# State space outputs behind twelve gate tiles, memory's norm behind all, projections sequence by sequence, lag 0 in one matmul with the other lags

## The chip, the cores and the metric

The kernel runs on one core of one Trainium2 chip. The metric is the device time of one execution in microseconds (us). A core has five engines, each with its own stream of instructions: TensorE (PE, the matmuls; PEld is its loading of weights), VectorE (DVE), ScalarE (ACT), GpSimd (POOL) and SyncE (SP, which here issues the transfers between HBM and the on-chip memory). An engine takes its instructions in order and waits on semaphores for what others produce.

## The reference

One encoder layer (DEPTH is 1) and a final norm, for two sequences ("prompt" and "sample", 512 tokens of 1024 features each) with a memory of 256 tokens each. The layer has three branches, a state space layer (S5), differential attention and cross attention over the memory; each goes through an up projection and a gate, their sum through an output projection; a gated feed-forward network follows.

```python
def _layer(x, mem, l, p):
    xn = _rmsnorm(x, p['norm_mix'][l])
    mn = _rmsnorm(mem, p['norm_mem'][l])
    h = xn @ p['w_in'][l]
    u, q, k, v, xq, g = jnp.split(h, IN_SPLITS, axis=-1)
    y_s5 = _s5_branch(u, ...)
    ...
    q = _partial_rope(q.reshape(Bn, L, 2 * DIFF_HEADS, DIFF_DH), cos, sin)
    k = _partial_rope(k.reshape(Bn, L, 2 * DIFF_HEADS, DIFF_DH), cos, sin)
    ...
    y_diff = _diff_attention(q, k, v, lam, p['diff_subln'][l], lambda_init)
    mk, mv = jnp.split(mn @ p['w_mem_kv'][l], 2, axis=-1)
    ...
    y_x = _cross_attention(xq.reshape(Bn, L, X_HEADS, X_DH), mk, mv)
    branches = (y_s5, y_diff, y_x)
    merged = None
    for n in range(N_BRANCH):
        term = jax.nn.sigmoid(g[..., n * D_MODEL:(n + 1) * D_MODEL]) * (branches[n] @ p['w_up'][l, n])
        merged = term if merged is None else merged + term
    x = x + merged @ p['w_out'][l]
    xn2 = _rmsnorm(x, p['norm_ffn'][l])
    gate, up = jnp.split(xn2 @ p['w_ffn_in'][l], 2, axis=-1)
    return x + (jax.nn.silu(gate) * up) @ p['w_ffn_out'][l]

def _s5_scan_dir(u, lam, step, b, c):
    lam_bar = jnp.exp(lam * step[:, None])
    b_bar = ((lam_bar - 1.0) / lam)[..., None] * b
    bu = jnp.einsum('lgh,gph->lgp', u.astype(jnp.complex64), b_bar)
    a = jnp.broadcast_to(lam_bar, bu.shape)
    _, xs = lax.associative_scan(_ssm_combine, (a, bu), axis=0)
    return jnp.real(jnp.einsum('lgp,ghp->lgh', xs, c))
```

The state space branch has 32 groups of 16 channels and 64 complex states, runs forward and backward in time, and ends with a gelu and a sigmoid gate of its own (w_glu).

## The kernel before, in words

**Precision.** All matrices are float32. For most products each operand is split into a high part (fp32r, which TensorE multiplies at full rate) and a low part, and three matmuls are made of one: low x with high weight, high with high, high x with low weight. `mm3` (lines 122 to 129) issues them for one slice k of 128 rows: for each sequence `xh` at line 126 and `xl` at line 127 with the weight's high part, then for each sequence line 129 with its low part. `weight` (lines 115 to 120) loads one 128x1024 tile of a weight matrix through a pool of two buffers; ScalarE makes the high part (line 109), VectorE the low part by a subtraction (line 110). `proj` (lines 131 to 137) makes one output tile of 128 features by 512 tokens for each of the two sequences: it takes two banks of PSUM, and in each step k it runs both sequences, three matmuls of 512 columns each. With 8 steps that is 48 matmuls for a tile of the gates or of the queries and keys, 24 for a tile of w_glu.

**The order of the stages.** Keys and values of the memory come first, then the norm of x and the input projection u of the state space branch (lines 277 to 291, written to memory and read back group by group). Then follow the gate tiles: 24 of them, each a `proj`, a tanh and a store (`gates`, lines 295 to 304). The state space branch is a Python generator, `s5_gen` (lines 893 to 1155); `next(s5)` issues its next stage between the gate tiles. `NG = (7, 10, 2)` says how many gate tiles stand between: seven, then memory's norm and the scan with its outputs, ten more, then the gelu of the state space outputs (lines 318 to 334), two more, then the four w_glu tiles (lines 338 to 346). The remaining five gate tiles stand in the attention stages (`NG_X`, `NG_D`). After w_glu come cross attention (lines 405 to 470), differential attention (`qk_tile`, lines 483 to 504, makes rotated queries and keys; `attend`, lines 506 to 546, one head of one sequence), the merging of the branches (`merge`, lines 551 to 599), the output projection, the feed-forward network (matmuls at lines 723 to 725) and the final norm. The attention stages take their projections' banks from two that are called mm, with three for scores and others for transposes (`open_banks` at the start of cross attention).

**What decides the order on an engine.** The program is built with a planner that simulates a timeline and moves instructions of one engine past one another where their data and buffers allow; the order of the Python code is its starting point, not the final order.

**Memory's norm** (lines 309 to 313): `sums` (lines 193 to 199) loads the four tiles of memN, squares them and sums them on TensorE; `factor` (lines 159 to 167) takes the square root on ScalarE, the reciprocal on VectorE (line 163), and spreads the four columns over the partitions by four transposes on TensorE (line 166); the results `mrs` and `mbc` are used in cross attention.

**The state space stages.** `cprod` (lines 1027 to 1035) makes complex products of a group's vectors with powers of its eigenvalues, six VectorE instructions for each block of eight groups. `input_weights` (lines 1038 to 1048) transposes them for the input matmuls. `output_weights` (lines 1056 to 1084) takes such products for eight lags in each direction (`Orf`, `Onf`, 128 columns a group), stores them in `cD`, and multiplies them on TensorE with the input vectors, which gives the kernel of the short-range lags: lines 1076 and 1077 make the 128 columns of the lags in plain float32, lines 1078 and 1079 the 16 columns of lag 0, from the vectors `cr` and `cn` themselves. The results go to `gD`. The scan (lines 1117 to 1123) carries the states over the 64 chunks of 8 tokens: 62 steps of four VectorE instructions. After it the outputs (lines 1125 to 1153): for each of four blocks of eight groups the stored products `c_r`, `c_n` and the lag matrix `w_` are loaded, ScalarE and VectorE copy a block's states into `x2` (one buffer), and TensorE makes 24 matmuls (lines 1146 to 1148), whose results are written to memory and read back by the gelu.

Of the kernel before, what the change touches and what calls it, by code (L numbers as in the profile page):

```python
# [10 lines left out]
F32 = mybir.dt.float32  # L11
# [24 lines left out]
NG = (7, 10, 2)  # L36
# [12 lines left out]
def encoder(ctx: ExitStack, tc: tile.TileContext, a, out):  # L49
# [34 lines left out]
    def bank(tag="mm"):  # L84
        return pools[tag].tile([P, 512], F32, tag=tag, name="bk" + tag)
# [35 lines left out]

    def mm3(outs, wh, wl, xs, k, nk):

        ws = slice(k * P, (k + 1) * P)
        for s, (xh, xl) in enumerate(xs):
            PE.matmul(outs[s], wh[:, ws], xh, start=(k == 0), stop=False)  # L126
            PE.matmul(outs[s], wh[:, ws], xl, start=False, stop=False)  # L127
        for s, (xh, xl) in enumerate(xs):
            PE.matmul(outs[s], wl[:, ws], xh, start=False, stop=(k == nk - 1))  # L129

    def proj(src, hi, lo, nk=KD, seqs=(0, 1)):

        wh, wl = weight(src, nk * P)
        outs = [bank() for _ in seqs]
        for k in range(nk):
            mm3(outs, wh, wl, [(hi[k][:, s * L : (s + 1) * L], lo[k][:, s * L : (s + 1) * L]) for s in seqs], k, nk)
        return outs
# [156 lines left out]

    def gates(n):

        for _ in range(n):
            t = next(todo)
            o = proj(a["w_in"][20 + t], xh, xl)
            gt = slot("ld", name="gt")  # L300
            for s in range(NS):
                cs = slice(s * L, (s + 1) * L)
                S.activation(out=gt[:, cs], in_=o[s], func=AF.Tanh, scale=0.5)
            nc.sync.dma_start(gD[t], gt)
# [3 lines left out]

    mrs = cst.tile([P, 4], F32, name="mrs")
    mbc = cst.tile([P, L], F32, name="mbc")  # L310
    rs_, bc = factor(sums(a["memN"], "ld"), DM)
    V.tensor_copy(mrs, rs_)
    S.copy(mbc, bc)
    next(s5)
    gates(NG[1])
    next(s5, None)
# [18 lines left out]
    gates(NG[2])  # L335
    bh = rp.tile([P, 4], F32, tag="bh", name="bh")
# [556 lines left out]
def s5_gen(k):  # L893
# [133 lines left out]
    def cprod(tag, ar, ai, xr, xi, sub):  # L1027

        o_r, o_i = slot(tag, sh4, name="cxr"), slot(tag, sh4, name="cxi")
        for o_, x1, x2, op in ((o_r, ar, ai, ALU.subtract if sub else ALU.add), (o_i, ai, ar, ALU.add if sub else ALU.subtract)):  # L1030
            t1 = slot(tag, sh4, name="ct1")
            V.tensor_tensor(out=t1, in0=x1, in1=xr, op=ALU.mult)
            V.tensor_tensor(out=o_, in0=x2, in1=xi, op=ALU.mult)
            V.tensor_tensor(out=o_, in0=t1, in1=o_, op=op)
        return tuple(o_.rearrange("p g e h -> p (g e h)") for o_ in (o_r, o_i))


    def input_weights(o):
        res = []
        for w_ in cprod("it", by_group(b_r, o), by_group(b_i, o), by_token(qr, o), by_token(qi, o), True):  # L1040
            t_ = slot("wb", [P, 8 * P], name="wb")
            for g4 in range(2):
                tr = aux()
                for g in range(4):
                    PE.transpose(tr[:, g * P : (g + 1) * P], w_[:, (4 * g4 + g) * P : (4 * g4 + g + 1) * P], ident)
                S.copy(t_[:, g4 * 512 : g4 * 512 + 512], tr)
            res.append(t_)
        return res
# [5 lines left out]
    cD = drp.tile([4, 2, P, 8 * 8 * 16], F32, name="cD")  # L1054

    def output_weights(o):
        Orf, Onf = cprod("it", by_group(cr, o), by_group(cn, o), by_token(xr_, o), by_token(xi_, o), False)
        nc.sync.dma_start(cD[o, 0], Orf)
        nc.sync.dma_start(cD[o, 1], Onf)
        for g4 in range(2):  # L1060
# [8 lines left out]
            for g2 in range(2):  # L1069
                kp = aux()  # L1070
                for g in range(2):
                    gg = 2 * g2 + g
                    lhr, lhi = lr48[:, gg, :], li48[:, gg, :]
                    cols = slice((4 * g4 + gg) * P, (4 * g4 + gg + 1) * P)
                    k1, k2 = kp[:48, g * 144 : g * 144 + P], kp[:48, g * 144 + P : (g + 1) * 144]
                    PE.matmul(k1, lhr, Orf[:, cols], start=True, stop=False)
                    PE.matmul(k1, lhi, Onf[:, cols], start=False, stop=True)
                    PE.matmul(k2, lhr, cr[:, hs.start + gg, :], start=True, stop=False)
                    PE.matmul(k2, lhi, cn[:, hs.start + gg, :], start=False, stop=True)
# [37 lines left out]
    for i in range(2, NC):  # L1117
# [5 lines left out]
        V.tensor_tensor(out=sv[:, :, :, i], in0=p_, in1=q_, op=ALU.add)  # L1123

    rt.close()
    k.open_tags(rt, side="right", x2=1, ow=6, sy=2)
    yv = k.yD.rearrange("(g h) j s c -> j h g (s c)", h=16)
    for o in range(4):
        gs = slice(8 * o, 8 * o + 8)
        c_r, c_n, w_ = (slot("ow", [P, 8, P], name=n_) for n_ in ("c_r", "c_n", "w_"))  # L1130
        nc.sync.dma_start(c_r.rearrange("p g q -> p (g q)"), cD[o, 0])
        nc.sync.dma_start(c_n.rearrange("p g q -> p (g q)"), cD[o, 1])
# [8 lines left out]
        for g4 in range(2):  # L1141
            ps = aux()
            for g in range(4):
# [3 lines left out]
                PE.matmul(d_, c_r[:, gg, :], x2[:, 0, 2 * gg : 2 * gg + 2, :].rearrange("p s c -> p (s c)"), start=False, stop=False)  # L1147
                PE.matmul(d_, c_n[:, gg, :], x2[:, 1, 2 * gg : 2 * gg + 2, :].rearrange("p s c -> p (s c)"), start=False, stop=True)
# [101 lines left out]
```

## Time and profile before

| What | Value |
|---|---|
| time, median of 3 runs | 1697.35 us (1695.62 to 1697.57) |
| time of the profiled execution | 1694.85 us |
| its span | 1693.0 us |
| mean granted clock of TensorE in it | 0.94 |
| moved by DMA | 196.66 MB, mean 116 GB/s |

The span runs from the first to the last instruction that the profiler recorded; the time has 1.85 us around it. "Granted clock" is the speed that the chip allowed TensorE, as a share of full speed. In the list of groups, a line such as "L126 PE MATMUL bkmm<-xh,wh 128x512 x640" names the line of the kernel, the engine, the operation, its output and inputs by the program's names, the shape, and how often it ran; behind the bar stand its summed busy time, the mean of one in ns, and the idle time of the engine just ahead of such instructions with what ended most of it. In a list of waits, "A <- B: 6.1, 4, 2.7" means that A waited for B for 6.1 us in all, in four waits, the longest 2.7. In a timeline each line begins with the start and the duration in us, and a bracket at its end gives the engine's idle time before it and what ended it. In a table by stretches, each line begins with the stretch and its length; then, for PE, PEld, DVE, ACT and POOL, the busy time and the number of instructions; then the mean granted clock, the share of the DMA engines' time and the GB/s moved.

### The profile page before, as it was taken

How to read it: one execution, taken by the hardware profiler on the slowest of the kernel's cores; microseconds unless marked ns; L12 is line 12 of the kernel's file. 1: busy time of each engine (PE TensorE's matmuls, PEld its weight loads, DVE VectorE, ACT ScalarE, POOL GpSimd, SP SyncE). 2: the span in 40 equal slices, each digit the busy share in tenths (PEclk: the TensorE clock that was granted, in tenths of full speed). 3: DMA queues.
4: the chain of work that ended last, by engine and by line, in shares of the span. 5: the costliest groups of instructions: out<-in, count | busy, mean ns of one | idle time of the engine just before them, and what ended most of it. 6: DMA issues, size and time to landing. Idle time of an engine off the chain costs nothing.

```text
span 1693.0 us, 21270 instructions
## 1 busy us (share of the span) xinstructions
PE 1631.7 (96%) x8044; PEld 1365.5 (81%) x8044; DVE 1086.8 (64%) x1788; ACT 620.1 (37%) x1092; POOL 391.0 (23%) x245
## 2 busy tenths in 40 slices
PE   5999998999999999999999999999999999999997
PEld 4788887887797778877888887888888888788887
DVE  7946897153554677778657659877777777753324
ACT  6534333243343446455422434222332323421121
POOL 0000000000000220210144345554555553500021
PEclk8999998999999999999999998999999999999998
DMA  9343262644112221315453541322222222742202
GB/s 363 112 151 117 92 211 103 197 176 174 47 51 75 69 69 51 112 46 160 154 188 119 152 134 63 112 100 88 75 88 75 88 87 98 237 148 66 77 22 100
DMA packets 79270, 196.66 MB, mean 116 GB/s; under 512 B 11072, under 2 KB 26688, under 8 KB 79168
## 3 DMA queue, kind: packets, MB, share of 16 engines
q1 hardware_dynamic: 79168, 195.31, 34.5%
q8 instruction: 63, 1.03, 0.3%
q14 instruction: 39, 0.32, 0.1%
HBM read 141.30 MB, written 49.77 MB: 113 GB/s over the span
## 4 chain that ended last, share of the span: by engine, by line
PE 67%; DVE 3%; ACT 2%; issue 1%; POOL 1%; DMA 1%; DVEq 0%; SPq 0%; POOLq 0%; ACTq 0%
PE bkmm L126 12%; PE bkmm L127 12%; PE bkmm L129 12%; PE bkmm L724 8%; PE bkmm L723 8%; PE bkmm L725 8%; DMA m<-m 1%; PE bksc L519 1%; PE bkmm L424 1%; PE bkmm L426 1%; PE bkmm L425 1%; PE bksc L520 1%; PE bktr L528 1%; POOL t L493 1%; DVE wl L110 0%
## 5 line engine op out<-in xcount | busy, mean ns | idle before, releaser
L109 ACT CAST wh<-wf 128x1024 fp32r<-128x1024 f32 (+4 forms) x164 | 142.3, 868 | 434.8 <-PE bkmm L127 278.8
L126 PE MATMUL bkmm<-xh,wh 128*128 128x512 f32 x640 | 252.8, 396 | 7.6 <-DVE t L491 3.0
L127 PE MATMUL bkmm<-xl,wh 128*128 128x512 f32 x640 | 251.8, 393 | 0.0
L724 PE MATMUL bkmm<-tl,wh 128*128 128x512 f32 x612 | 239.6, 391 | 2.9 <-DVE tl L110 2.9
L110 DVE TENSOR_TENSOR wl<-wf,wh 128x1024 fp32r<-128x1024 f32 (+4 forms) x164 | 182.5, 1113 | 92.0 <-ACT wh L109 91.1
L723 PE MATMUL bkmm<-th,wh 128*128 128x512 f32 x612 | 239.4, 391 | 0.0
L725 PE MATMUL bkmm<-th,wl 128*128 128x512 f32 x612 | 237.9, 390 | 0.0
L129 PE MATMUL bkmm<-xh,wl 128*128 128x512 f32 x640 | 224.1, 394 | 0.0
L126 PEld LDWEIGHTS bkmm<-xh,wh 128*128 128x128 f32 x640 | 120.9, 189 | 35.5 <-DVE t L491 5.5
L127 PE MATMUL bkmm<-al,wh 128*128 128x512 f32 (+1 forms) x408 | 147.0, 360 | 0.0
L126 PE MATMUL bkmm<-ah,wh 128*128 128x512 f32 (+1 forms) x408 | 147.0, 360 | 0.0
L492 POOL TENSOR_TENSOR t<-t,rs 128x512 f32<-128x512 f32 x16 | 21.9, 1368 | 518.1 <-DVE t L491 430.9
L127 PEld LDWEIGHTS bkmm<-xl,wh 128*128 128x128 f32 x640 | 121.1, 189 | 24.3 <-issue 0.2
L129 PEld LDWEIGHTS bkmm<-xh,wl 128*128 128x128 f32 x640 | 120.5, 189 | 24.4
L724 PEld LDWEIGHTS bkmm<-tl,wh 128*128 128x128 f32 x612 | 115.5, 189 | 28.4 <-DVE tl L110 4.6
L723 PEld LDWEIGHTS bkmm<-th,wh 128*128 128x128 f32 x612 | 115.5, 189 | 24.4 <-ACT th L109 0.3
L725 PEld LDWEIGHTS bkmm<-th,wl 128*128 128x128 f32 x612 | 115.1, 188 | 23.7
L129 PE MATMUL bkmm<-ah,wl 128*128 128x512 f32 (+1 forms) x408 | 127.4, 360 | 1.0 <-DVE wl L110 1.0
L788 POOL TENSOR_TENSOR up<-up,acc 128x512 f32<-128x512 f32 x44 | 85.1, 1956 | 148.0 <-DVE up L764 148.0
L848 DVE TENSOR_TENSOR y<-y,bkmm 128x512 f32<-128x512 f32 (+1 forms) x56 | 32.6, 609 | 110.8 <-PE bkmm L129 110.8
L146 POOL TENSOR_TENSOR acc<-acc,nsq 128x512 f32<-128x512 f32 (+1 forms) x32 | 37.9, 1186 | 242.4 <-ACT nsq L145 242.3
L129 PEld LDWEIGHTS bkmm<-ah,wl 128*128 128x128 f32 x408 | 76.9, 189 | 13.2 <-DVE wl L110 1.8
(586 smaller groups left out, 3293.9 us busy)
## 6 DMA issues: line engine op xcount, KB each, us to landing
wf<-in_w_in SPq DMA_DIRECT2D x40, 512.0 KB, 3.5
gD<-gt SPq DMA_DIRECT2D x24, 512.0 KB, 2.9
gl<-gD SPq DMA_DIRECT2D x24, 512.0 KB, 4.2
wf<-in_w_fg SPq DMA_DIRECT2D x22, 512.0 KB, 3.3
wf<-in_w_fu SPq DMA_DIRECT2D x22, 512.0 KB, 3.3
aD<-ac SPq DMA_DIRECT2D x22, 512.0 KB, 2.6
fl<-aD SPq DMA_DIRECT2D x22, 512.0 KB, 4.6
wf<-in_w_fo SPq DMA_DIRECT2D x16, 448.0 KB, 3.3
```

The lines of the kernel that those rows point to most:

```text
L109: S.copy(hi, src)
L110: V.tensor_tensor(out=lo, in0=src, in1=hi.bitcast(F32), op=ALU.subtract)
L126: PE.matmul(outs[s], wh[:, ws], xh, start=(k == 0), stop=False)
L127: PE.matmul(outs[s], wh[:, ws], xl, start=False, stop=False)
L129: PE.matmul(outs[s], wl[:, ws], xh, start=False, stop=(k == nk - 1))
L146: eng.tensor_tensor(out=acc[:, :n], in0=acc[:, :n], in1=sq[:, :n], op=ALU.add)
L492: PO.tensor_tensor(out=t2, in0=t2, in1=rope[1], op=ALU.mult)
L723: PE.matmul(ps, wh[:, ws_], th[:, o], start=(k == 0), stop=False)
L724: PE.matmul(ps, wh[:, ws_], tl[:, o], start=False, stop=False)
L725: PE.matmul(ps, wl[:, ws_], th[:, o], start=False, stop=(k == 3))
L788: PO.tensor_tensor(out=up, in0=up, in1=accs[s], op=ALU.mult)
L848: V.tensor_tensor(out=y[m][:, c : c + n], in0=y[m][:, c : c + n], in1=o_, op=ALU.add)
```

## The change

Five things are edited.

1. `proj` finishes the first sequence's eight steps before it begins the second's, and takes each bank when its sequence begins. The matmuls of a tile are the same in number.
2. `NG` becomes (7, 5, 7). The generator stops once more, after the scan, and its outputs are issued after twelve gate tiles, inside `with behind():`. `behind` returns `tc.issue_after(last_mm.ins)`: the instructions issued inside it may not be put ahead of the last matmul of the last `proj` before it. Seven gate tiles follow; in the code the gelu stands ahead of them.
3. Memory's norm moves from behind the seventh gate tile to behind all nineteen, also inside `behind()`.
4. Lag 0 is joined to the other lags. The product tiles of `output_weights` get a ninth slot of 16 columns for each group, into which GpSimd copies `cr` and `cn`; one pair of matmuls of 144 columns takes the place of a pair of 128 and a pair of 16. `cD`, `c_r` and `c_n` are 144 columns wide, and the output matmuls read their first 128.
5. `x2` has two buffers in place of one.

```diff
-NG = (7, 10, 2)
+NG = (7, 5, 7)
...
+    last_mm = None
     def mm3(outs, wh, wl, xs, k, nk):
+        nonlocal last_mm
         ws = slice(k * P, (k + 1) * P)
         for s, (xh, xl) in enumerate(xs):
             PE.matmul(outs[s], wh[:, ws], xh, start=(k == 0), stop=False)
             PE.matmul(outs[s], wh[:, ws], xl, start=False, stop=False)
         for s, (xh, xl) in enumerate(xs):
-            PE.matmul(outs[s], wl[:, ws], xh, start=False, stop=(k == nk - 1))
+            last_mm = PE.matmul(outs[s], wl[:, ws], xh, start=False, stop=(k == nk - 1))
     def proj(src, hi, lo, nk=KD, seqs=(0, 1)):
         wh, wl = weight(src, nk * P)
-        outs = [bank() for _ in seqs]
-        for k in range(nk):
-            mm3(outs, wh, wl, [(hi[k][:, s * L : (s + 1) * L], lo[k][:, s * L : (s + 1) * L]) for s in seqs], k, nk)
+        outs = []
+        for s in seqs:
+            cs = slice(s * L, (s + 1) * L)
+            outs.append(bank())
+            for k in range(nk):
+                mm3(outs[-1:], wh, wl, [(hi[k][:, cs], lo[k][:, cs])], k, nk)
         return outs
...
+    def behind():
+        return tc.issue_after(last_mm.ins)
...
     next(s5)
     gates(NG[0])
-
-    mrs = cst.tile([P, 4], F32, name="mrs")
-    mbc = cst.tile([P, L], F32, name="mbc")
-    rs_, bc = factor(sums(a["memN"], "ld"), DM)
-    V.tensor_copy(mrs, rs_)
-    S.copy(mbc, bc)
     next(s5)
     gates(NG[1])
+    with behind():
+        next(s5)
     next(s5, None)
...
     gates(NG[2])
+    with behind():
+        mrs = cst.tile([P, 4], F32, name="mrs")
+        mbc = cst.tile([P, L], F32, name="mbc")
+        rs_, bc = factor(sums(a["memN"], "ld"), DM)
+        V.tensor_copy(mrs, rs_)
+        S.copy(mbc, bc)
...
-        o_r, o_i = slot(tag, sh4, name="cxr"), slot(tag, sh4, name="cxi")
-        for o_, x1, x2, op in ((o_r, ar, ai, ALU.subtract if sub else ALU.add), (o_i, ai, ar, ALU.add if sub else ALU.subtract)):
+        tiles = [slot(tag, [P, 8, 8 if sub else 9, 16], name=n_) for n_ in ("cxr", "cxi")]
+        for o_, x1, x2, op in ((tiles[0], ar, ai, ALU.subtract if sub else ALU.add), (tiles[1], ai, ar, ALU.add if sub else ALU.subtract)):
+            o_ = o_[:, :, 0:8, :]
             t1 = slot(tag, sh4, name="ct1")
             V.tensor_tensor(out=t1, in0=x1, in1=xr, op=ALU.mult)
             V.tensor_tensor(out=o_, in0=x2, in1=xi, op=ALU.mult)
             V.tensor_tensor(out=o_, in0=t1, in1=o_, op=op)
-        return tuple(o_.rearrange("p g e h -> p (g e h)") for o_ in (o_r, o_i))
+        return tiles
     def input_weights(o):
         res = []
         for w_ in cprod("it", by_group(b_r, o), by_group(b_i, o), by_token(qr, o), by_token(qi, o), True):
+            w_ = w_.rearrange("p g e h -> p (g e h)")
...
-    cD = drp.tile([4, 2, P, 8 * 8 * 16], F32, name="cD")
+    cD = drp.tile([4, 2, P, 8, 144], F32, name="cD")
     def output_weights(o):
         Orf, Onf = cprod("it", by_group(cr, o), by_group(cn, o), by_token(xr_, o), by_token(xi_, o), False)
+        PO.tensor_copy(Orf[:, :, 8, :], cr[:, 8 * o : 8 * o + 8, :])
+        PO.tensor_copy(Onf[:, :, 8, :], cn[:, 8 * o : 8 * o + 8, :])
+        Orf, Onf = (o_.rearrange("p g e h -> p g (e h)") for o_ in (Orf, Onf))
         nc.sync.dma_start(cD[o, 0], Orf)
         nc.sync.dma_start(cD[o, 1], Onf)
...
-                    cols = slice((4 * g4 + gg) * P, (4 * g4 + gg + 1) * P)
-                    k1, k2 = kp[:48, g * 144 : g * 144 + P], kp[:48, g * 144 + P : (g + 1) * 144]
-                    PE.matmul(k1, lhr, Orf[:, cols], start=True, stop=False)
-                    PE.matmul(k1, lhi, Onf[:, cols], start=False, stop=True)
-                    PE.matmul(k2, lhr, cr[:, hs.start + gg, :], start=True, stop=False)
-                    PE.matmul(k2, lhi, cn[:, hs.start + gg, :], start=False, stop=True)
+                    k1 = kp[:48, g * 144 : (g + 1) * 144]
+                    PE.matmul(k1, lhr, Orf[:, 4 * g4 + gg, :], start=True, stop=False)
+                    PE.matmul(k1, lhi, Onf[:, 4 * g4 + gg, :], start=False, stop=True)
                 S.copy(gk[:, 2 * g2 : 2 * g2 + 2, :].rearrange("p g c -> p (g c)"), kp[:48, : 2 * 144])
...
         V.tensor_tensor(out=sv[:, :, :, i], in0=p_, in1=q_, op=ALU.add)
+    yield
     rt.close()
-    k.open_tags(rt, side="right", x2=1, ow=6, sy=2)
+    k.open_tags(rt, side="right", x2=2, ow=6, sy=2)
     yv = k.yD.rearrange("(g h) j s c -> j h g (s c)", h=16)
     for o in range(4):
         gs = slice(8 * o, 8 * o + 8)
-        c_r, c_n, w_ = (slot("ow", [P, 8, P], name=n_) for n_ in ("c_r", "c_n", "w_"))
-        nc.sync.dma_start(c_r.rearrange("p g q -> p (g q)"), cD[o, 0])
-        nc.sync.dma_start(c_n.rearrange("p g q -> p (g q)"), cD[o, 1])
+        c_r, c_n = (slot("ow", [P, 8, 144], name=n_) for n_ in ("c_r", "c_n"))
+        w_ = slot("ow", [P, 8, P], name="w_")
+        nc.sync.dma_start(c_r, cD[o, 0])
+        nc.sync.dma_start(c_n, cD[o, 1])
...
-                PE.matmul(d_, c_r[:, gg, :], x2[:, 0, 2 * gg : 2 * gg + 2, :].rearrange("p s c -> p (s c)"), start=False, stop=False)
-                PE.matmul(d_, c_n[:, gg, :], x2[:, 1, 2 * gg : 2 * gg + 2, :].rearrange("p s c -> p (s c)"), start=False, stop=True)
+                PE.matmul(d_, c_r[:, gg, 0:P], x2[:, 0, 2 * gg : 2 * gg + 2, :].rearrange("p s c -> p (s c)"), start=False, stop=False)
+                PE.matmul(d_, c_n[:, gg, 0:P], x2[:, 1, 2 * gg : 2 * gg + 2, :].rearrange("p s c -> p (s c)"), start=False, stop=True)
```

## The prediction, made before the changed kernel was run

> **What bounds the kernel now.** I read the page first, then the list of what PE waited for, then the timeline and stretches around the changed stages. Section 1, and the granted clock of section 2:
>
> ```profile
> PE 1631.7 (96%) x8044; PEld 1365.5 (81%) x8044; DVE 1086.8 (64%) x1788; ACT 620.1 (37%) x1092; POOL 391.0 (23%) x245
> PEclk8999998999999999999999998999999999999998
> ```
>
> TensorE (PE) is the bound: it is idle for only 61 us of 1693.0. A gain is therefore PE work taken away, a PE wait removed, or half-clock time avoided. The page shows 128x512 matmuls of 390 ns, but these overlap: in a full stretch they start every 0.227 us (925 to 1000 us holds 333). I use 0.227. What PE waited for, over the whole run (us, times, longest):
>
> ```profile
> PE bksc L519 <- DMA m<-m: 6.1, 4, 2.7
> PE bktr L166 <- DVE rs L163: 5.8, 3, 4.6
> PE bkmm L126 <- DVE t L491: 3.0, 5, 1.0
> ...
> PE bkmm L126 <- ACT sg L342: 1.3, 1, 1.3
> PE bkmm L126 <- DVE r L359: 1.2, 1, 1.2
> ```
>
> The 4.6 us is the memory norm (lines 309 to 313). PE's timeline there, then the stretches in which the clock was granted at half:
>
> ```profile
> 258.73 1.09 PE L166 MATMUL bktr<-ident,rs 128*128 128x128 f32 x4 [4.56 <-DVE rs L163]
> ```
>
> ```profile
> 256.89:263.70 6.81, 4.97 (x17) 4.42 (x18) 6.57 (x20) 0.59 (x1) 0.00 (x0) 0.50 0.22 77
> 434.38:437.78 3.40, 3.40 (x11) 2.72 (x11) 2.40 (x11) 1.02 (x4) 0.00 (x0) 0.50 0.46 159
> 762.06:765.46 3.40, 3.23 (x8) 2.29 (x9) 3.40 (x6) 3.00 (x4) 0.00 (x0) 0.50 0.77 229
> ```
>
> The reader sees that an idle stretch is paid twice: 4.56 us of waiting, then 4.97 us of work at clock 0.50 instead of 0.95, which is 4.97 x (1 - 0.50/0.95) = 2.4 us lost.
>
> **The change, part by part.** The order of both programs' instructions is the same up to the first lag matmuls (118 us) and again from the output projection on (920 us). Only the stretch between can change; the rest, 890 us, is taken as it is.
>
> *Lag 0 joined to the other lags (old lines 1074 to 1079).* One visit of PE to these matmuls, with the gate matmul after it:
>
> ```profile
> 212.51 0.42 PE L1076 MATMUL bktr<-cxr,lr 128*48 128x128 f32 x2
> 212.77 0.39 PE L1077 MATMUL bktr<-cxi,li 128*48 128x128 f32 x2
> 212.99 0.22 PE L1078 MATMUL bktr<-cr,lr 128*48 128x16 f32 x2
> 213.07 0.24 PE L1079 MATMUL bktr<-cn,li 128*48 128x16 f32 x2
> 213.16 0.40 PE L1076 MATMUL bktr<-cxr,lr 128*48 128x128 f32 x2
> ...
> 214.93 0.24 PE L1079 MATMUL bktr<-cn,li 128*48 128x16 f32 x2
> 215.10 0.50 PE L126 MATMUL bkmm<-xh,wh 128*128 128x512 f32 x1
> 215.44 0.39 PE L127 MATMUL bkmm<-xl,wh 128*128 128x512 f32 x1
> ```
>
> Each plain float32 matmul is two records. The two 16-column matmuls of a group cost 213.16 - 212.99 = 0.17 us, and there are 32 groups: 5.4 us go. The remaining 128 records grow from 128 to 144 columns; a record takes (212.99 - 212.77)/2 = 0.11 us, so an eighth is 0.014 us, and 128 of them 1.8 us. Net -3.6 us, on the path, because PE has no idle time from 118 to 250 us. Added are eight small copies on GpSimd (128x128 elements). The trace has none; the nearest rows are its memset of 128x192 (0.26 us, L1064) and its 128x512 sums (1.3 to 2.2 us, L492 and L493), so 0.3 to 0.6 us each. GpSimd is busy for 3.2 us of 118 to 254, so they hide, unless one stands ahead of a matmul that already waits (then 0.6 us each, 5 us at the worst). The sixteen transfers of cD grow by an eighth; landing takes 2.6 to 6.1 us, so 0.8 us more at most, hidden by loads that are issued tens of us ahead.
>
> *Fewer changes between kinds of matmul.* In the rows above, the first gate matmul after the visit holds PE for 215.44 - 215.10 = 0.34 us instead of 0.227, the last L1079 pair 0.17 instead of 0.09, and the edge before the visit costs about as much again in its two halves (0.09 and 0.04): 0.32 us a visit. Counting visits in the two orders, 219 changes of kind become 209, mostly because the output matmuls (lines 1146 to 1148) now stand in two blocks behind the twelfth and in the fourteenth gate tile, where before they were cut into about eight pieces. Five visits less: -1.6 us.
>
> *Memory's norm behind all gate tiles.* Its four transposes move into the second w_glu tile; with them go four loads of memN, four squares and two table loads on ScalarE, and a reciprocal. The wait of 4.6 and the half clock of 2.4 us go: -6.9. In the new place the square root follows the first half of the first w_glu output, and the transposes stand some 6.5 us of PE work behind that: table load 1.28, root 0.30, reciprocal 0.18, about 3 us to spare. Queued behind the loads on SP are the last gate's store and the fourth w_glu weight, which has 12 us of cover. Without that cover it would cost the same 4.6 again.
>
> *What the stall was hiding.* The scan (lines 1120 to 1123) fills VectorE from 182.6 to 282.7, and between its steps VectorE makes the low halves of the gate weights (L110):
>
> ```profile
> 257.06 1.22 DVE L110 TENSOR_TENSOR wl<-wf,wh 128x1024 fp32r<-128x1024 f32 x1
> ...
> 270.58 1.21 DVE L110 TENSOR_TENSOR wl<-wf,wh 128x1024 fp32r<-128x1024 f32 x1
> ```
>
> They come 13.5 us apart, while a gate tile is 48 x 0.227 = 10.9 us of PE. PE did not run into this because it stood still for the norm at 254. In the new order PE works without a break, so it does. The weight of the eleventh gate tile stands behind 17 more scan instructions (0.36 us each) and one more L110 (1.02 us net) than the one that started at 257.06: it starts at about 264.4 and is ready at 265.6. PE wants it at 264.7 (the last scan input ends at 181.4, then 82.9 us of PE work to that tile, then two matmuls): 0.9 late. The twelfth follows 34 scan instructions and one L110 later, ready at 278.8; PE wants it at 275.6 + 0.9: 2.2 more. So +3.1 us, from 0 (scan begins 3 us earlier) to 6 (3 us later). Next behind these: the outputs. The scan ends near 284 and its two copies (1.9 and 1.2 us) by 286; PE arrives near 289, so the outputs wait for nothing. Their own old waits for each other and for w (0.3 + 0.7) go: -0.7.
>
> *Projections one sequence, then the other.* Matmuls and weight loads are the same in number. What moves is when the first half is ready: 24 x 0.227 = 5.4 us earlier. At the start of cross attention PE waited for sg (1.27, bank not yet free), for qh (1.21) and for ql (0.52); counted in matmuls, the new order leaves 5.4 us between the first half and the first score, and over 2 us for the bank. So -3.0. The half clock at 434.38 followed those waits: 3.40 x 0.47 = -1.6, of which I take -1.0. In differential attention the waits on L491 and r (3.0 + 1.2) are two projections meeting at two banks; the shortest distances there are 0.2 to 1.9 us before, 0.9 to 1.9 after, and only three of them: -4.2. The score waits on the key's transfers (6.1) I leave as they are: bounds below.
>
> The Trainium skill's page "TensorE: Matmul & The Clock Gate" (section "HAM oscillation — how this bites in real kernels") says that the clock falls back after an idle stretch of about 3.4 us. This trace agrees at 4.56 us, but shows the half clock also at 434.38 and 762.06, where the longest single idle before it was 1.3 and 1.8 us. By the page alone the -1.0 would not be had and the sum would be 1 us smaller.
>
> **Sum.** -3.6 - 1.6 - 6.9 + 3.1 - 0.7 - 3.0 - 1.0 - 4.2 = -17.9 us. The profiled execution took 1694.85 us, a span of 1693.0; the new span would be 1675. The median of the runs shown is 1697.35, 2.5 above the profiled one; against it the forecast is 1679.5.
>
> **Rivals.** (a) The order by sequences does nothing in the attention stages: before, the trace at 609 to 614 us already runs L126, L127, L129 once each, so the planner had split the sequences wherever a bank was missing. For it: exactly that row. Against: the first cross projection was not split. The 4.2 stay: 1683.7. (b) VectorE paces the gates: the scan's lateness is 6 instead of 3.1, and its short idles gather into a half-clock stretch like the first above (6.81 x 0.47 = 3.2): 1685.6. Against: idles of 1 to 2 us, 11 us apart. (c) Slower: the key chain keeps its length while the planner moves the scores forward. Before, the first scores of the four heads stood 10.9, 16.0, 13.9 and 12.2 us of PE work behind their key projection and waited 0.9, 2.3, 0.2 and 2.7, so the chain took 11.8, 18.3, 14.1 and 14.9. Now they stand 10.9, 10.7, 10.2 and 9.2 behind. With the old lengths they wait 18.1 instead of 6.1, +12.0, three of the four long enough to halve the clock for 3 to 7 us (+6.0), and the 4.2 fall away: -17.9 + 22.2 = +4.3, so 1701.7. It decides once these waits exceed 24 us. Against: the 18.3 held 6 us in VectorE's queue and a transfer of 5.1 us behind a weight load; the bare chain (0.6, 0.7, 1.3, 2.2, 0.6, 2.3) is 8 us. (d) Better: the key waits vanish as well: 1673.4.
>
> **How the numbers follow.** Forecast 0.42, (a) 0.22, (b) 0.16, (c) 0.12, (d) 0.08. The range 1667 to 1697 takes in all but (c); its low end is (d) with the lateness at 0 and no more half clock at 762, its high end is (b) with the copies at 5 us and the key waits 6 us longer. A measurement of this kernel can tell 0.2%, 3.4 us, from no change: the upper ends of the forecast and of (b) (0.04) and the lower end of (c) (0.01) lie within it. Faster 0.84, same 0.05, slower 0.11.
>
> **What would show it.** No wait of L166 on L163 near 254 and no half clock there; L1078 and L1079 without successors; PE waiting for wl (L110) by 1 to 3 us between 264 and 280; the outputs in two blocks from about 289; no wait for sg or qh near 420 to 435. It is wrong if the score waits on m grow past 12 us, if the new transposes wait, or if new half-clock stretches stand between 430 and 860.

## The result, and the profile after

The changed kernel takes 1674.72 us (median of 4 runs, 1673.46 to 1675.12); the kernel before, in the runs beside it, 1696.48 us (4 runs, 1694.43 to 1697.57). The ratio is 0.9872, with a 95% interval of 0.9855 to 0.9889. The profiled execution took 1674.95 us, a span of 1673.2, 19.8 us less than the 1693.0 of before. The forecast was 1679.5 us, a gain of 17.9.

The page of the changed kernel, engines and granted clock:

```profile
PE 1625.6 (97%) x7916; PEld 1357.8 (81%) x7916; DVE 1076.2 (64%) x1788; ACT 622.1 (37%) x1092; POOL 391.7 (23%) x253
PEclk9999999999999999999999999999999999999999
```

TensorE has 128 records fewer, the L1078 and L1079 that lag 0 had. The row of the clock prints a 9 for anything from 90%; the finer table by stretches looks as if the chip had run faster, 0.95 before and 1.00 after. It did not. From 1100 to 1200 us both kernels are in the feed-forward network (columns: the stretch, its length, then busy time and instructions of PE, PEld, DVE, ACT, POOL, then granted clock, DMA share, GB/s), before:

```profile
1100.00:1200.00 100.00, 100.00 (x443) 82.80 (x442) 76.74 (x90) 29.25 (x36) 56.96 (x33) 0.95 0.26 90
```

and after:

```profile
1100.00:1200.00 100.00, 100.00 (x443) 82.77 (x442) 76.75 (x90) 29.89 (x37) 53.96 (x33) 1.00 0.24 85
```

443 matmuls in 100 us in both, at "0.95" and at "1.00". Only the stretches at 0.50 mean time here; the full value differs from one execution to the next.

What TensorE waited for in the changed kernel (us in all, times, longest):

```profile
PE bkmm L132 <- DVE wl L110: 3.4, 3, 1.9
...
PE bksc L533 <- ACT e L371: 2.3, 4, 1.5
PE bksc L533 <- DMA m<-m: 2.2, 3, 1.1
...
PE bkmm L129 <- DVE t L505: 1.2, 2, 0.6
PE bktr L1165 <- DMA w__2771<-gD: 1.1, 1, 1.1
PE bkmm L129 <- DVE vl L110: 1.0, 1, 1.0
```

The wait for the norm (rs, 4.6) is gone, those of the scores for m fell from 6.1 to 2.2, those for t from 3.0 to 1.2. New are two waits for wl, 3.0 of the 3.4; the one for w was 0.7 before. (The names: wl is the low half of a weight; m the rotated keys, half of which a transfer moves to other partitions; t the rotation that reads a projection's bank and so frees it; r and e the reciprocal and the exponentials of a softmax; vl the low half of the values; x and w a block's states and lag matrix at the state space outputs.) The start times of the same instructions in the two timelines of TensorE give the stages:

| Stage | Before, us | After, us | Difference | Forecast |
|---|---|---|---|---|
| start to the first lag matmul | 111.8 | 110.9 | -0.8 | 0 |
| to the last w_glu matmul | 298.7 | 292.2 | -6.5 | -9.7 |
| to the first cross attention score | 14.1 | 11.1 | -3.0 | -3.0 |
| to the first score of differential attention | 135.6 | 131.9 | -3.7 | -5.2 for this and the next two rows |
| to the last such score | 244.5 | 236.7 | -7.8 | |
| to the output projection | 107.9 | 107.9 | 0.1 | |
| to the end | 765.6 | 767.2 | 1.6 | 0 |

The first row runs the same matmuls in the same order, and so does the last but for eight matmuls at the start of the output projection; over all kernels of this document the last row takes 765.6 to 767.2 us, in the old order and in the new, so these differences are from one execution to the next. The stages are read from one profiled execution of each kernel, the times from all of its runs. So the total was near, but its parts were not: the state space stretch gave 3.2 us less than forecast, attention 6.2 us more.

### The profile page after: what moved, and what is told of

Same layout as the page of the kernel before. It is cut to its first block, busy times and chain, and to the rows that moved or that the text cites. A ratio compares the mean times of both kernels' runs of the same rounds, so it can differ in the third digit from the quotient of the medians.

```text
span 1673.2 us, 21052 instructions
## 1 busy us (share of the span) xinstructions
PE 1625.6 (97%) x7916; PEld 1357.8 (81%) x7916; DVE 1076.2 (64%) x1788; ACT 622.1 (37%) x1092; POOL 391.7 (23%) x253
## 4 chain that ended last, share of the span: by engine, by line
PE 79%; DVE 11%; DMA 3%; issue 2%; ACT 2%; POOL 1%; SPq 1%; DVEq 0%; POOLq 0%; ACTq 0%
PE bkmm L129 15%; PE bkmm L132 15%; PE bkmm L130 15%; PE bkmm L738 8%; PE bkmm L737 8%; PE bkmm L739 8%; DVE st L1140 1%; DVE wl L110 1%; PE bktr L1122 1%; POOL mg L587 1%; PE bksc L533 1%; DMA c_n<-cD 1%; PE bksc L534 1%; PE bkmm L438 1%; PE bkmm L439 1%
## 5 line engine op out<-in xcount | busy, mean ns | idle before, releaser
L132 PE MATMUL bkmm<-xh,wl 128*128 128x512 f32 x640 | 252.1, 394 | 3.0 <-DVE wl L110 3.0
L110 DVE TENSOR_TENSOR wl<-wf,wh 128x1024 fp32r<-128x1024 f32 (+4 forms) x164 | 175.7, 1072 | 94.5 <-ACT wh L109 93.9
```

The lines of the kernel that those rows point to most:

```text
L110: V.tensor_tensor(out=lo, in0=src, in1=hi.bitcast(F32), op=ALU.subtract)
L132: last_mm = PE.matmul(outs[s], wl[:, ws], xh, start=False, stop=(k == nk - 1))
```

## The experiments

Each kernel was timed in five rounds beside the kernel before; "ratio" is to the kernel before on the same chip. First the edits one at a time; the second buffer of x2 goes with the held outputs and is not timed apart from them.

**Lag 0 alone.** Edit, as in the diff above:

```diff
+        PO.tensor_copy(Orf[:, :, 8, :], cr[:, 8 * o : 8 * o + 8, :])
...
-                    PE.matmul(k2, lhr, cr[:, hs.start + gg, :], start=True, stop=False)
-                    PE.matmul(k2, lhi, cn[:, hs.start + gg, :], start=False, stop=True)
...
```

> The kernel before, with only lag 0 joined to the other lags. Theory: 128 records of 16 columns fewer and an eighth more columns in the others is worth 3.6 to 4.3 us on TensorE's path, all of it between the first and the last lag matmul (95.1 us before, about 91 here): 1692 to 1693 us in all. Rival: GpSimd's copies stand ahead of matmuls, or the planner answers the change elsewhere; then that stretch shrinks and another grows by as much, and the time stays within 2 us of before.

Measured: 1691.14 us against 1694.37, ratio 0.9982 (0.9973 to 0.9991). Between the first and the last lag matmul 93.5 us pass instead of 95.1, with 12 more gate matmuls among them (12 x 0.227 = 2.7 us), so the edit gave 4.3 us there (3.9 against five other kernels with the old lag matmuls, in which the stretch takes 94.75 us). From there to w_glu, 1.4 us went back: TensorE comes to the outputs earlier and waits 1.8 us there for x and 1.2 for w (before: 0.3 for the matmuls ahead and 0.7 for w), while the norm's wait fell only from 4.6 to 3.7. The theory's size holds; the net is 3 us because the scan does not end earlier.

**Projections by sequences alone.**

```diff
-        outs = [bank() for _ in seqs]
-        for k in range(nk):
-            mm3(outs, wh, wl, [(hi[k][:, s * L : (s + 1) * L], lo[k][:, s * L : (s + 1) * L]) for s in seqs], k, nk)
+        outs = []
+        for s in seqs:
+            cs = slice(s * L, (s + 1) * L)
+            outs.append(bank())
+            for k in range(nk):
+                mm3(outs[-1:], wh, wl, [(hi[k][:, cs], lo[k][:, cs])], k, nk)
```

> The kernel before, with only the projections run one sequence, then the other. Theory: all of the gain between the last w_glu matmul and the last score matmul (14.4 us) is due to this edit: 1682 to 1684 us, the waits for m fall from 6.1 us to 2 or 3 and those of the projections for VectorE's t from 3.0 to about 1.2. Rival: the shorter waits in attention come from where the planner put the gate tiles and weight loads once the other edits were in; then only the 3.0 us at the start of cross attention go, 1693 us, and the waits for m stay near 6.

Measured: 1689.42 us, ratio 0.9968 (0.9952 to 0.9985). Neither expectation: the start of cross attention gave its 3.0 us and the stage behind it 3.6 (1.6 of these are a half-clock stretch of the kernel before that comes and goes, see below), but from the first score of differential attention to the output projection the time is 352.1 us against 352.4. Its waits:

```profile
PE bkmm L126 <- DVE vl L110: 3.4, 1, 3.4
PE bksc L523 <- DMA m<-m: 2.7, 2, 1.7
PE bktr L1151 <- ACT x L1142: 2.4, 1, 2.4
```

The waits for m did fall (6.1 to 2.7), but in this kernel's order of instructions one for vl grew from 2.1 to 3.4, and there are half-clock stretches at 639 and 663 us. So the order by sequences alone is not what saved 7.8 us there.

**Memory's norm alone.**

```diff
-    rs_, bc = factor(sums(a["memN"], "ld"), DM)
...
     gates(NG[2])
+    with behind():
...
+        rs_, bc = factor(sums(a["memN"], "ld"), DM)
```

> The kernel before, with only memory's norm moved behind all gate tiles. Theory: the wait of 4.6 us and the half clock behind it (2.4) go, and VectorE's lateness with the low halves of the gate weights, which the stall had hidden, comes up in its place (two waits for wl between 260 and 282 us, 3.0 together): 3 to 5 us faster, 1692 to 1693 us. Rival: the lateness in the changed kernel belongs to the outputs that are held back or to the order by sequences; then no wait for wl shows here and the full 6.9 us are had, 1689 to 1690 us.

Measured: 1696.31 us against 1694.37, ratio 1.0008 (1.0000 to 1.0017). Both theories missed: one wait for wl of 1.0 us came, and a longer one, for the scan's end, behind it. TensorE's timeline and VectorE's, at the place where the outputs begin:

```profile
283.64 0.79 PE L1156 MATMUL bktr<-x,c_r 128*128 128x128 f32 x2 [5.78 <-ACT x L1147]
```

```profile
281.28 0.37 DVE L1132 TENSOR_TENSOR st<-p__2348,q__2349 128x128 f32<-128x128 f32 x1
281.74 1.23 DVE L1148 COPY x<-st 64x2048 f32<-64x2048 f32 x1
```

The scan ends at 281.7 us, about as before (282.7), and the outputs that the planner put here cannot begin sooner: a stall of 4.6 us for the norm became one of 5.8 us for the scan, and a half-clock stretch of 6.8 us stands there too. The norm's wait was idle time that the scan needed anyway.

**Outputs held alone.**

```diff
-NG = (7, 10, 2)
+NG = (7, 5, 7)
...
+    with behind():
+        next(s5)
...
+    yield
...
-    k.open_tags(rt, side="right", x2=1, ow=6, sy=2)
+    k.open_tags(rt, side="right", x2=2, ow=6, sy=2)
```

> The kernel before, with only the outputs held behind twelve gate tiles (7, 5, 7) and two buffers of x2; memory's norm stays at its old place with its wait of 4.6 us. Theory: fewer visits to the output matmuls (8 changes of kind fewer, 1.3 us) and their waits for each other gone (0.3): 1 to 2 us faster. Rival: holding them only moves the wait for w (0.7 before, 1.1 in the changed kernel) and gives nothing: within 1 us of before.

Measured: 1692.11 us, ratio 0.9984 (0.9975 to 0.9993), 2.7 us by the ratio. The stretch up to w_glu is 2.4 us shorter: the outputs' own waits went (0.3 and 0.7 us), and the half-clock stretch at 257 us is 3.4 us long instead of 6.8, worth 1.0 (its matmuls lose 1.4 us to it instead of 2.4). The norm's wait ahead of it stays (4.7 us), so it isn't shown that the edit shortened that stretch. The expectation's size was nearly right, its reason (visits) was not: see below.

The four ratios multiply to 0.9942; the changed kernel's is 0.9872. More than half of the gain is thus in combinations, which two pairs tell apart.

**Lag 0 and projections together, nothing else.**

> The kernel before, with lag 0 joined and the projections by sequences, and nothing else. In the built program its order of matmuls from the first cross attention score to the output projection is that of the changed kernel, while each of the two edits alone gives an order of its own. Theory: the gain in the attention stages that neither edit had alone (about 7.7 us between the first score of differential attention and the output projection) comes from this pair: 1678 to 1681 us, with a part of the lag gain given back before w_glu in a longer wait for the scan's end (x, 2 to 4 us). Rival: the parts add up, 0.3 and 0.2%: 1686 us.

Measured: 1677.28 us against 1695.42, ratio 0.9904 (0.9887 to 0.9922). From the first score of differential attention to the output projection it takes 344.9 us, as the changed kernel (344.7), where each edit alone took 352.1 and 353.2. Its waits:

```profile
PE bktr L1162 <- ACT x L1153: 3.4, 1, 3.4
...
PE bksc L530 <- DMA m<-m: 2.2, 3, 1.1
...
PE bkmm L129 <- DVE vl L110: 1.0, 1, 1.0
```

All of the attention gain is here, and 3.4 us are given back at the scan's end (x), as foreseen. Lag 0 touches nothing in attention; what the two edits do as a pair is to give the planner a program from which it makes another order there. The profiles of all kernels of this document bear this out: they show five orders of TensorE's matmuls in attention. Four of these, in nine kernels, take 352.1 to 355.8 us from the first score of differential attention to the output projection; the fifth, which the changed kernel, this one and the two last ones below share, takes 344.4 to 345.1.

**Norm and outputs together, nothing else.**

> The kernel before, with memory's norm behind all gate tiles and the outputs held behind twelve, and nothing else. Theory: neither is of use alone, because the stretch up to w_glu ends with the scan on VectorE, and the stall only changes its place (4.6 us at the norm, 5.8 us at the outputs' states); together the wait goes, and what is left is VectorE's lateness with the gate weights (wl, 3 us) and a half-clock stretch: 4 to 6 us faster than before, 1688 to 1690 us, order in attention unchanged. Rival: the parts add up (0.1% slower and 0.16% faster): 1693 us.

Measured: 1688.52 us, ratio 0.9964 (0.9950 to 0.9978). From the last lag matmul to the last of w_glu it takes 198.3 us against 203.6. Its waits:

```profile
PE bksc L530 <- DMA m<-m: 6.6, 3, 2.9
PE bkmm L129 <- DVE t L502: 3.0, 5, 1.0
PE bkmm L132 <- DVE wl L110: 2.6, 2, 1.4
```

The stall is gone, what is left of it is the lateness of wl, and the order in attention is untouched (m and t nearly as before). No half-clock stretch follows the waits for wl here. The two pairs' ratios multiply to 0.9868, within the interval of the changed kernel's 0.9872: between the pairs nothing is left to explain.

Then the changed kernel with one edit undone, and the kernel itself on the same chip:

> The changed kernel itself, for comparison on the same chip: 0.987 of the time before, 1673 to 1675 us.

Measured: 1675.42 us, ratio 0.9884 (0.9872 to 0.9897).

**Without lag 0's joining:**

```diff
-        PO.tensor_copy(Orf[:, :, 8, :], cr[:, 8 * o : 8 * o + 8, :])
...
+                    PE.matmul(k2, lhr, cr[:, hs.start + gg, :], start=True, stop=False)
+                    PE.matmul(k2, lhi, cn[:, hs.start + gg, :], start=False, stop=True)
```

> The changed kernel without the joining of lag 0 (the other edits are in). Its order of matmuls in attention is that of the kernel with the projection edit alone. Theory: beside the 4.2 us of the lag matmuls it loses what the two edits have only as a pair, 6 to 8 us in attention: 1684 to 1687 us. Rival: the joining is worth its own matmuls only: 1678 to 1679 us.

Measured: 1683.90 us, ratio 0.9933 (0.9922 to 0.9945), 8.5 us behind the changed kernel timed beside it. The stage from the first to the last score of differential attention and on to the output projection takes 353.0 us instead of 345.1, and the wait for vl is 3.4 us again: the theory.

**Without the order by sequences:**

```diff
-        outs = []
-        for s in seqs:
-            cs = slice(s * L, (s + 1) * L)
-            outs.append(bank())
-            for k in range(nk):
-                mm3(outs[-1:], wh, wl, [(hi[k][:, cs], lo[k][:, cs])], k, nk)
+        outs = [bank() for _ in seqs]
+        for k in range(nk):
+            mm3(outs, wh, wl, [(hi[k][:, s * L : (s + 1) * L], lo[k][:, s * L : (s + 1) * L]) for s in seqs], k, nk)
```

> The changed kernel with the projections back in the interleaved order (the other edits are in). Its order of matmuls in attention is that of the kernel with the lag edit alone. Theory: the order by sequences carries the 3.0 us at the start of cross attention and, with the pair's 7.7 and 1 to 3 us more, nearly all of the gain behind w_glu: 1686 to 1689 us. Rival: the planner's new order carries it, whichever way the projections run: 1677 to 1680 us.

Measured: 1687.57 us, ratio 0.9956 (0.9944 to 0.9968). Its waits:

```profile
PE bksc L529 <- DMA m<-m: 6.2, 3, 2.7
PE bkmm L129 <- DVE t L501: 2.2, 3, 1.0
```

The waits for m and t are nearly those of before: the theory.

**Without the order by sequences in the queries and keys alone:**

```diff
+        if old:
+            outs = [bank() for _ in seqs]
...
-        o = proj(a["w_in"][mt], xh, xl)
+        o = proj(a["w_in"][mt], xh, xl, old=True)
```

> The changed kernel, with the eight query and key projections of differential attention alone back in the interleaved order. Theory: these are the ones whose order counts there; a key's first half comes 5.4 us later and its transfers meet those of the second half, so the waits for m go back from 2.2 to 5 us or more, and the time grows by 5 to 8 us, to 1680 to 1683. Rival: what the planner made of the whole counts, not the key's own order: the waits for m stay at 2 to 3 us and the time within 3 us of the changed kernel.

Measured: 1682.57 us against 1695.42, ratio 0.9924 (0.9910 to 0.9938). Its waits:

```profile
PE bksc L538 <- DMA m<-m: 4.1, 3, 2.3
PE bkmm L129 <- DVE t L510: 3.2, 5, 1.0
```

The time is the theory's, the reason only in part: the waits for m went to 4.1 us, not to 5 or more, and those for t, two projections meeting at two banks, came back whole (3.2). So did waits that are no part of the theory, vl (2.1) and e of the softmax (1.7), and the stage up to the output projection takes 353.6 us, as in the other old orders. As this edit gives the planner yet another order, the causes are not separated further.

Last, two kernels on the lateness of wl, the new wait.

**Low halves on GpSimd:**

```diff
+POOL_LOW = (8, 9, 10, 11)
...
-            o = proj(a["w_in"][20 + t], xh, xl)
+            o = proj(a["w_in"][20 + t], xh, xl, eng=PO if t in POOL_LOW else V)
```

> The changed kernel, with the low halves of the weights of gate tiles nine to twelve made on GpSimd instead of VectorE (four 128x1024 subtractions). Theory: VectorE paces the gate tiles during the scan, 13.5 us a tile against 10.9 us of matmuls; with 4.4 us of VectorE's work gone the two waits for wl (3.0 us) and the half-clock stretch behind them (1.7) vanish: 1670 to 1671 us. Rival: GpSimd's subtraction takes so long, or slows VectorE's scan so much, that TensorE waits for wl as before or for the scan's end: 1673 to 1678 us.

Measured: 1678.87 us against 1695.42, ratio 0.9904 (0.9891 to 0.9918), 3 to 4 us slower than the changed kernel by the medians, though its interval just touches that of the changed kernel's second measurement, 0.9884. No wait for wl is left among the gate tiles. GpSimd's timeline, then VectorE's:

```profile
231.79 2.50 POOL L111 TENSOR_TENSOR wl<-wf,wh 128x1024 fp32r<-128x1024 f32 x1 [27.14 <-ACT wh L110]
```

```profile
231.71 0.39 DVE L1138 TENSOR_TENSOR p__2100<-st,l8r 128x128 f32<-128x128 f32 x1
232.01 2.45 DVE L1139 TENSOR_TENSOR q__2101<-st,l8i 128x128 f32<-128x128 f32 x1
234.38 0.38 DVE L1140 TENSOR_TENSOR p__2100<-p__2100,st 128x128 f32<-128x128 f32 x1
```

A scan instruction that takes 0.38 us elsewhere takes 2.45 here, from its start until GpSimd's subtraction is done. So each subtraction on GpSimd costs the scan about 2.1 us of blocking, while the same subtraction on VectorE costs it 1.2 us less some 0.2 of overlap. Four of them: the scan ends at 287.4 us instead of 283.0, and TensorE waits for it:

```profile
289.42 0.51 PE L1167 MATMUL bktr<-x,c_r 128*128 128x128 f32 x2 [3.95 <-ACT x L1158]
```

Behind that it also waits for w, 1.4 and 2.6 us, where the changed kernel waited 1.1, and two half-clock stretches of 3.4 us follow these waits where the changed kernel had one.

The Trainium skill's page "SBUF — State Buffer" (section "SBUF: two separate sides") says that VectorE with two inputs in SBUF and GpSimd share a pair of ports, which whoever comes first holds for its whole instruction. This trace agrees, in all four places (2.45 to 2.56 us).

**The order of VectorE alone:**

```diff
+CUT = (50, 57)
...
-    gates(NG[1])
+    gates(NG[1] - 1)
+    with tc.issue_after(last_low.ins):
+        next(s5)
+    gates(1)
+    with tc.issue_after(last_low.ins):
+        next(s5)
...
     for i in range(2, NC):
+        if i in CUT:
+            yield
```

Here `last_low` is the instruction of line 110 that came last, so the rest of the scan stands behind it.

> The changed kernel, with the order of VectorE alone altered: the low halves of the weights of gate tiles eleven and twelve stand behind 192 and 220 instructions of the scan instead of 200 and 234; no work is added or taken. Theory: PE's two waits for wl (3.0 us) and the half clock behind them (1.7) are only a matter of this order, as the scan ends some 7 us before its outputs are wanted: the waits go, the scan still ends at about 283 us, and the time is 4 to 5 us less than the changed kernel's, 1669 to 1671 us. Rival: the stretch is bound by the scan, so that what is won at wl comes back as a wait for x or for w at the outputs, as when GpSimd made the low halves: within 1.5 us of the changed kernel.

Measured: 1672.25 us (4 runs, 1671.18 to 1673.69) beside 1675.42 (4 runs, 1674.73 to 1676.07) for the changed kernel; ratio 0.9864 (0.9849 to 0.9878). Between the two expectations. The waits for wl are gone, but two for w stand in their place, where the changed kernel had one of 1.1 to 1.4 (in its two profiles):

```profile
309.83 0.46 PE L1176 MATMUL bktr<-u__1186,w__2718 128*128 128x128 f32 x2 [2.23 <-DMA w__2718<-gD]
317.60 0.46 PE L1176 MATMUL bktr<-u__1186,w__2771 128*128 128x128 f32 x2 [2.17 <-DMA w__2771<-gD]
```

SP's queue in the same kernel:

```profile
308.74 5.90 SPq L1165 DMA_DIRECT2D w__2771<-gD  x8
```

The eight transfers of a block's w are issued over 5.9 us. Each takes SP only 0.3 to 0.44 us, but the last is held back by 2.0, for a reason that the profile does not show; those of the block before (w__2718) are cut apart by stores of y and issued over 15.5 us. A half-clock stretch of 3.4 us stands at 319 us, behind these waits. So by the profile the rival holds: from the first lag matmul to the last of w_glu this kernel takes 292.1 us, the changed kernel 292.2 and 293.0 in its two profiles. The two timed ranges do not overlap, but the intervals of the two ratios do, and the profiled spans are only 1.0 us apart (1671.9 and 1672.9): that this kernel beats both is likely, its 3 us are not settled.

## Why the prediction was right in sum and wrong in parts

That the total came near is in part luck: two errors, 3.2 us too much in the state space stretch and 6.2 too little in attention, have opposite signs.

**Right: lag 0, in kind.** Forecast -3.6, measured -4.2 (95.07 to 92.42 us, with 7 more gate matmuls of 0.227 in it), or -3.9 against the 94.75 us of five other kernels. GpSimd's copies took up to 1.35 us, not 0.3 to 0.6, but TensorE waited for none of them.

**Right: the norm's wait and what it hid.** The 4.6 us and the half clock behind it went, the transposes wait for nothing in the w_glu tiles, and VectorE's lateness came up where and as large as worked out, 0.9 and 2.2 us forecast. (The 181.4 us from which it was worked out stand in no row; the last input matmul of the scan ends at 180.1.) TensorE after:

```profile
265.03 0.50 PE L132 MATMUL bkmm<-xh,wl 128*128 128x512 f32 x1 [1.08 <-DVE wl L110]
...
278.13 0.50 PE L132 MATMUL bkmm<-xh,wl 128*128 128x512 f32 x1 [1.92 <-DVE wl L110]
```

VectorE after, the two low halves, still 13 us apart:

```profile
263.76 1.21 DVE L110 TENSOR_TENSOR wl<-wf,wh 128x1024 fp32r<-128x1024 f32 x1
276.86 1.22 DVE L110 TENSOR_TENSOR wl<-wf,wh 128x1024 fp32r<-128x1024 f32 x1
```

What the prediction did not say is that the norm edit is worth nothing without the held outputs; it counted the outputs as an edit of their own, -1.6 and -0.7, while their main use is to let the norm's gain through.

**Wrong: the half clock behind the lateness.** Only rival (b) had one. The stretches after:

```profile
279.35:282.76 3.41, 3.41 (x9) 2.63 (x9) 3.24 (x11) 0.00 (x0) 0.00 (x0) 0.50 0.36 135
...
256.89:263.70 6.81, 6.81 (x32) 5.51 (x30) 6.50 (x20) 1.00 (x2) 0.00 (x0) 1.00 0.00 0
434.38:437.78 3.40, 3.40 (x22) 3.01 (x21) 1.14 (x1) 2.15 (x4) 0.00 (x0) 1.00 0.00 0
```

The two old places are clean; a new one, 9 matmuls in 3.41 us, follows the wait of 1.92. It costs 1.6 us, and it stands in both profiles of the changed kernel.

**Wrong: the visits, -1.6.** The price of a change of kind was read off single rows (0.34 instead of 0.227 us). Between the last lag matmul and the last of w_glu the changes fell from 13 to 7; summing each matmul's start to the next one's start at full clock and without waits, the excess over 0.227 and 0.11 us is 1.3 us before and after. Over all kernels of this document it is 1.0 to 1.4 us with 13 changes and 0.7 to 1.5 with 7. The visits were worth nothing that shows: the excess of single rows does not add up to time over the stretch.

**Wrong: the outputs' waits, -0.7.** Their old waits went, but one for w came (1.1 us): +0.1.

**Right: the start of cross attention**, -3.0 forecast and measured.

**Not shown: its half clock.** The stretch at 434 us, of which the forecast took 1.0 of 1.6, is gone. But six kernels with the old start of cross attention have the same three waits there, 1.27, 1.21 and 0.52 us, and in only two of them, the kernel before and the changed one without the order by sequences, does a half-clock stretch follow. The same place in the kernel with the outputs held alone:

```profile
430.00:433.41 3.41, 3.41 (x17) 2.88 (x17) 2.41 (x11) 1.02 (x4) 0.00 (x0) 1.00 0.45 159
```

So up to 1.6 us of what attention gave came with the one execution of the kernel before that was profiled, and are not shown to be the edit's; that the forecast's -1.0 was had is luck.

**Wrong: the rest of attention.** Forecast -4.2 for t and r, and nothing for m ("I leave as they are"). Measured: t and r fell by 3.0, m by 3.9, e (L525) by 1.4, vl by 1.1, and the half-clock stretch at 762 us is not there (between 748 and 772 us one begins in seven of the nine kernels with the old orders and in none with the new); waits of scores for e grew by 1.3. (The prediction would have counted a new half-clock stretch between 430 and 860 us against itself. The second profile of the changed kernel has one, at 535 us; the stage that it stands in takes 131.9 us with it and without it.)

Rival (d) was right for 3.9 of its 6.1 us, rival (a) wrong about t and r, which fell with the order by sequences alone too, and rival (c) wrong: the key chain did not keep its length. From the first read of the key's bank to the landing of m it took 8.0, 11.5, 7.9 and 11.1 us (15.0 to the second transfer) in the four heads before, and 7.9, 7.2, 7.0 and 7.2 after. What had made it long was SP's queue, here before, at the fourth head:

```profile
762.20 0.32 SPq L564 DMA_DIRECT2D gl<-gD  x1
762.62 0.47 SPq L501 DMA_DIRECT2D m<-m  x1
763.93 0.33 SPq L564 DMA_DIRECT2D gl<-gD  x1
764.35 0.47 SPq L501 DMA_DIRECT2D m<-m  x1
```

and after:

```profile
739.70 1.11 SPq L515 DMA_DIRECT2D m<-m  x2
```

Before, loads for the merges stood between the key's transfers, and these took 4.1 and 6.2 us to land; after, the two follow each other and land in 2.2.

That is a matter of where the planner puts the loads, and the pair of runs shows that lag 0 and the projections' order set the order in attention together. That the loads' place in the queue is what counts in it is read from the timelines, not tried by itself. The prediction credited attention to the projections alone. Why the width of lag 0's matmuls makes the planner choose otherwise some 400 us later was not tried.

**The range.** Its low end is said to be (d) with no lateness and no half clock at 762 us; that is 1673.4 - 3.1 - 1.6 = 1668.7, not 1667.

**The sum.** State space stretch 3.2 too much, attention 6.2 too little, and 0.8 lost in the unchanged ends from one execution to the next: 17.9 - 3.2 + 6.2 - 0.8 = 20.1 us from the first matmul to the last, 19.8 in the profiled spans, 21.8 in the medians. The profiled execution of the kernel before was one of its faster ones, 1694.85 us against the median of 1696.48.

## What to carry to other kernels

A wait can stand in for another: before pricing its removal, ask which long chain on another engine (here the scan on VectorE) ends next, and move the consumers of that chain in the same step. Where a planner sets the order, one edit measured alone tells little: compare the built orders first, group the variants that share one, and time the combinations. An engine that is idle is not free if it blocks the one that it should relieve.

## What the hardware showed unexpectedly

A GpSimd subtraction of 128x1024 (2.4 to 2.5 us) holds up a VectorE instruction on other data for its whole length (2.45 us instead of 0.38). The full value of the granted clock differs between executions, 0.949 in the profile of the kernel before and 1.0 in all others here, at the same pace of 443 matmuls in 100 us. Half-clock stretches last 3.4 us or a multiple of it (up to 13.7; the last one of a profile ends with it) and also follow clusters of waits of 1 to 2 us, but not always: the waits of 1.27, 1.21 and 0.52 us at the start of cross attention are followed by one in two of six profiles, and the same changed kernel shows one at 535 us in one execution and none in another. The Trainium skill's page "TensorE: Matmul & The Clock Gate" (section "Part 1: The HAM clock gate (the "warmup" mystery)") says that activity is judged in windows of about 3.4 us that run freely, so that where they fall varies from run to run; the lengths of 3.41 us and the stretch at 535 us agree.
